# First attention: two of four key blocks turned by VectorE and DRAM, and twelve weight units split on GpSimd during the first up-projection

## The chip, the cores and the metric

One core of a Trainium2 chip. The metric is the time of one execution of the program in microseconds (us); lower is better. The engines are called by their names in the profile: PE (TensorE, the matrix unit; PEld is its weight loads), DVE (VectorE), ACT (ScalarE), POOL (GpSimd) and SP (SyncE, which here only issues DMAs). SBUF is the on-chip memory of 128 partitions, PSUM holds the results of matmuls, DRAM is the memory off the core.

## What is computed

One layer of an encoder over two batches of 512 tokens ("prompt" and "sample"), width 1024: half a SwiGLU feed-forward, a mixing block (attention beside an mLSTM memory, merged by gates), half a second feed-forward, and a norm.

```python
def encoder_layer(x, cos, sin, ...):
    x = x + 0.5 * swiglu(rms_norm(x, ffn1_norm), ffn1_w_gate, ffn1_w_up, ffn1_w_down)
    h = rms_norm(x, mix_norm)
    proj = h @ w_in
    aq, ak, av, mq, mk, mv, gate_pre, o_pre, g_att, g_mlstm = jnp.split(proj, split_at, axis=-1)
    aq = apply_rope(rms_norm(aq.reshape(B, S, ATT_HEADS, ATT_HEAD_DIM), q_norm), cos, sin)
    ak = apply_rope(rms_norm(ak.reshape(B, S, ATT_KV_HEADS, ATT_HEAD_DIM), k_norm), cos, sin)
    att = gqa_block_attention(aq, ak, av)      # softmax(q k^T / 8) v: 8 heads of 64, 2 key/value heads
    mem = mlstm_bidirectional(mq, mk, mv, gate_pre, mlstm_gate_bias, o_pre, mlstm_head_norm)
    merged = jax.nn.sigmoid(g_att) * (att @ w_up_att) + jax.nn.sigmoid(g_mlstm) * (mem @ w_up_mlstm)
    x = x + merged @ w_out
    return x + 0.5 * swiglu(rms_norm(x, ffn2_norm), ffn2_w_gate, ffn2_w_up, ffn2_w_down)
```

Everything is float32. The feed-forward's inner width is 2816, which the kernel cuts into 22 blocks of 128.

## The kernel before

**Number format.** A float32 operand is split into a rounded high part and the rest, its low part; a product is then three matmuls (high by high, high by low, low by high). The split of a tile takes two instructions: one that writes the high part (ACT, L278, L332, L715) and a subtraction that writes the low part (DVE, L279, L333, L716).

**Stages.** In the trace of before: a prologue to about 84 us; the first up-projection (`Up.rest`, its products at L374) from 84 to 437; the first down-projection to 652; the mixing block, first for the prompt (s = 0), then for the sample (s = 1); and the second feed-forward from about 1390 to the end. The first attention (prompt) runs from 705 to 813, the second (sample) from about 1081 to 1187.

**Order of work.** The order of PE's matmuls is the order of the program, pinned. The other engines' instructions are put in order by a scheduler from priorities, and each engine then takes its own list strictly in that order, waiting on semaphores. DMAs are issued from SP's list, and some from POOL's.

**First up-projection.** Both batches go through it together: each block of the 22 is made of seven products, each of twelve matmuls (L374), except that for every second block two of the products were made and kept earlier. So its pattern repeats every two blocks. DVE forms sums and differences of weights (L355), splits them (L333, L716), and reads the products' sums out of PSUM (L413, L418); the raw weights come by SP (L271). Its tiles come from a ring with several named groups; the group "o" has seven tiles, which hold outputs until they are joined. POOL has hardly any work here: `mix_gains`, called after block 13, loads the gains of the norms.

**Weight units of the mixing block.** `in_w` is used in units of 1024 x 128 (512 KB). `load_w` (L285) brings a unit for the first batch raw (SP, L271), splits it by ACT (L278) and DVE (L279) into a pair of high and low tiles, and writes both to DRAM ("wpark", two DMAs of SP at L303). For the second batch it reads the two parts back (two DMAs, L293), with no split. A unit's matmuls are handed out in steps ("fillers") between the pieces of the attention: `among(n)` issues n steps (their lines are L825, L839 and L804).

**First attention.** Head by head (8), and in a head four passes, b = 0 to 3, one for each block of 128 queries. A pass makes for the next head the score (PE, L1101, 128 queries x 512 keys), its maximum (DVE, L1104), the exponential (ACT, L1106) and the scaling by the reciprocal of the sum (ACT, L1109, or DVE, L1111). For the present head it turns one block of 128 keys with `turn_keys`: four transposes of 128x128 on PE (L1117) into PSUM, which `parts` splits (ACT L715, DVE L716), for two matmuls with the values (L1148) one pass later. The second attention does so with two of the four key blocks only. The other two (key blocks 0 and 1) are turned by DVE in blocks of 32x32 (`turn_early`, L1129) into a tile "box", sent to DRAM by SP (`send`, L1133: four DMAs of 128 KB), and fetched in the turned order by POOL (`fetch`, L1138), two passes or more later; the blocks come in the order 2, 3, 0, 1.

Of the kernel before, what the change touches and what calls it, by code (L numbers as in the profile page):

```python
# [8 lines left out]
F32 = mybir.dt.float32  # L9
F32R = mybir.dt.float32r  # L10
I32 = mybir.dt.int32
AF = mybir.ActivationFunctionType
ALU = mybir.AluOpType
# [3 lines left out]
P = 128  # L17
S = 512
D = 1024
KD = D // P  # L20
# [6 lines left out]
def encoder(ctx, tc, I, outs):  # L27
    nc = tc.nc
    cpool = ctx.enter_context(tc.tile_pool(name="cpool", bufs=1))
    dpool = ctx.enter_context(tc.tile_pool(name="dpool", bufs=1, space=bass.MemoryType.DRAM))  # L30
# [11 lines left out]
    def nm(s):  # L42
        n_id[0] += 1
        return f"{s}_{n_id[0]}"

    @contextmanager
    def shifted(n):

        tc.cur_priority += n
        yield  # L50
        tc.cur_priority -= n
# [31 lines left out]
    class Rings:  # L83
# [11 lines left out]
        def rest(self, kind):  # L95

            rows = self.rows[kind]
            i = self.at[kind] % len(rows)
            return rows[i:] + rows[:i]
# [184 lines left out]
    parked = {}  # L284
# [24 lines left out]
    G_ = nc.gpsimd  # L309
    HK_ = KD // 2  # L310
# [156 lines left out]
    class Up:  # L467
# [13 lines left out]
        def fetch(self, j, which=(0, 1), behind=None):  # L481
            return [fetch_w(self.v[i][:, :, j * P:(j + 1) * P], behind) for i in which]
# [18 lines left out]
        def left(self, j):  # L501
            return gu_left_a(self.fetch(j, (0,))[0])

        def rest(self, raw, at=None, hook=None):
            ring = self.ring

            def resume(j):
                got = ring("v"), ring("h")
                for t, d in zip(got, self.kept.pop(j)):
                    nc.sync.dma_start(t, d)  # L510
                return got

            left = gu_left_b(*raw, ring)
            left.update(gu_left_c(raw[1], ring))
            raw = self.fetch(self.order[1])
            got = resume(self.order[0])
            for i, j in enumerate(self.order):
                W = left
                nxt = self.order[i + 1] if i + 1 < NF else None
                if nxt is not None:  # L520
                    left = {} if nxt in self.kept else gu_left_a(raw[0])
                    left.update(gu_left_b(*raw, ring))
                    ru = raw[1]
                    raw = self.fetch(self.order[i + 2]) if i + 2 < NF else None
                then = []
                h = gu_rest(W, self.xc, got, ring, lambda: then.append(resume(nxt)) if nxt in self.kept else None)
                got = then[0] if then else None
                if nxt is not None:
                    left.update(gu_left_c(ru, ring))
                if i % 2 == 0:  # L530
                    sides = Sides(self.rb[i // 2], ring)
                    with shifted(LATER):
                        sides.even(*h)
                elif i < NF - 1:
                    sides.odd(*h)
                if i == at:
                    hook(h[0])
            ring.join("o", "o", "wd")
            return lambda: sides.odd(*h)

# [178 lines left out]
    HA, HK, DA = 8, 2, 64  # L719
    HM, DM = 4, 128  # L720
# [44 lines left out]
    win_v = w_in.rearrange("(k p) c -> p k c", p=P)  # L765
# [82 lines left out]
    def mix(s, xh, xl, early=None, extra=None, after=None):  # L848
# [248 lines left out]
        def score(h, b):  # L1097
            hk = h // 4
            p = PS()
            for j in range(2):  # L1100
                pin(nc.tensor.matmul(p, qT[:, h, b * P:(b + 1) * P], kv[:, hk * 2 + j, :],  # L1101
                                     start=(j == 0), stop=(j == 1)))
            c = small(3, "asm")
            V_.tensor_reduce(c[:, 0:1], p, axis=AX.X, op=ALU.max, negate=True)  # L1104
            e = T2()
            nc.scalar.activation(e, p, AF.Exp, bias=c[:, 0:1], accum_out=c[:, 1:2])  # L1106
            V_.reciprocal(c[:, 2:3], c[:, 1:2])
            if b % 2 and (s or h or b < 3):
                nc.scalar.activation(e, e, AF.Copy, scale=c[:, 2:3])  # L1109
            else:  # L1110
                V_.tensor_scalar(e, e, c[:, 2:3], None, op0=ALU.mult)  # L1111
            return e

        def turn_keys(Ps, kb):
            p = PT()
            for b in range(4):
                pin(nc.tensor.transpose(p[:, b * P:(b + 1) * P], Ps[b][:, kb * P:(kb + 1) * P], ident))  # L1117
            return parts(p.rearrange("p (i a m) -> p a i m", i=4, a=4) if s else p)

        def parts(p):  # L1120
            ph, pl = T2(F32R), T2(F32R)
            v = (lambda t: t.rearrange("p (a i m) -> p a i m", i=4, a=4)) if len(p.shape) > 2 else lambda t: t
            split(p, v(ph), v(pl))
            return ph, pl
# [3 lines left out]
        def turn_early(t, b):  # L1128
            V_.transpose(turned[:, :, b, :], t[:, 0:2 * P].rearrange("p (n m) -> p n m", m=32))  # L1129
# [6 lines left out]
        def fetch(h, kb):  # L1136
            p = F2()
            nc.gpsimd.dma_start(p, abuf[h % 2][4 * kb:4 * kb + 4].rearrange("c r a x -> (c r) (a x)"))  # L1138
            return parts(p)

        pos = {}
        KBS = (2, 3, 0, 1) if s else (0, 1, 2, 3)

        def values(h, kb, pp):
            if kb == KBS[0]:
                pos[h] = PO()
            for i, w in enumerate(pp):
                pin(nc.tensor.matmul(pos[h], Vst[:, kb, h // 4, :], w, start=(kb == KBS[0] and i == 0),  # L1148
                                     stop=(kb == KBS[3] and i == 1)))
            if kb != KBS[3]:  # L1150
                return
            po = pos.pop(h)
            order = ((lambda t: t.rearrange("p (a i m) -> p i a m", i=4, a=4)),
                     (lambda t: t.rearrange("p (i a m) -> p i a m", i=4, a=4))) if s else (lambda t: t,) * 2
            if h % 2 == 0:
                afs[0] = T2(F32, "f2")
            af = afs[0]
            o0 = (h % 2) * DA
            o1 = DA - o0
            t = T2(F32, "f2")  # L1160
            was, now = order
            nc.scalar.activation(now(t[o0:o0 + DA, :]), was(po[o1:o1 + DA, :]), AF.Copy)
            V_.tensor_tensor(now(af[o0:o0 + DA, :]), was(po[o0:o0 + DA, :]), now(t[o0:o0 + DA, :]), op=ALU.add)
            if h % 2:
                split(af, att[:, h // 2, 0, :], att[:, h // 2, 1, :])
# [18 lines left out]
        Ps = []  # L1184
        rope = q_rope(1)
        for b in range(4):
            Ps.append(score(0, b))
            next(rope, None)
            among(FIRST[b])
        if s:  # L1190
            for i in range(2):
                turn_early(Ps[i], i)
        last = None
        for h in range(HA):
            nxt = []
            for b in range(4):
                if h in (0, 2, 4) and b == 2:
                    q_turn(h // 2 + 1, pin)
                if (h, b) == (0, 1):
                    gate_tops(*tops)  # L1200
                if (h, b) in ((0, 3), (2, 3)):
                    rope = q_rope(h // 2 + 2)
                if h < 4:
                    next(rope, None)
                if h + 1 < HA:
                    nxt.append(score(h + 1, b))
                if s and (h, b) != (HA - 1, 3) and b in (3, 0):
                    if b == 3:
                        for i in range(2):
                            turn_early(nxt[i], i)  # L1210
                    else:
                        for i in range(2, 4):
                            turn_early(Ps[i], i)
                if s and b == 1:
                    send(h)
                n0, n1_ = FILLER if b else SOON
                among(n0)
                pp = None
                if not s or b > 1:
                    pp = h, b, turn_keys(Ps, b)  # L1220
                elif h:
                    pp = h - 1, b, fetch(h - 1, b)
                among(n1_)
                if last:
                    values(*last)
                last = pp
                if extra and b == 2 and h in (2, 3, 4):
                    extra[h - 2]()
            Ps = nxt
        for b in range(2 * s):  # L1230
            pp = HA - 1, b, fetch(HA - 1, b)
            among(sum(FILLER))
            values(*last)
            last = pp
# [145 lines left out]
        if s:  # L1380
# [3 lines left out]
            at = [mem_blocks(0, mem_head(0))]  # L1384
# [71 lines left out]
    up = Up(xc, I["ffn1_w_gate"][0], I["ffn1_w_up"][0], rbuf[0], 12)  # L1456
# [245 lines left out]
    for k in range(HK_):  # L1702
# [10 lines left out]
        if k == 2:  # L1713
            raw0 = up.fetch(up.order[0])
# [2 lines left out]
    up.begun()  # L1717


    tail = up.rest(raw0, 13, mix_gains)  # L1720
    accs = [None, None]
    nhl = [None, None]
    box()
# [89 lines left out]
    up = Up(xc, I["ffn2_w_gate"][0], I["ffn2_w_up"][0], rbuf[1], 10)  # L1813
    raw0 = up.fetch(0)
# [20 lines left out]
    tail = up.rest(raw0)  # L1835
# [120 lines left out]
```

## Time and profile before

The median of three runs is 2034.01 us (2033.39 to 2034.31). The execution that was profiled took 2037.6 us, and its span, from the first to the last instruction recorded, is 2035.8 us, at a granted PE clock of 0.999.

| engine | busy us | share of the span | instructions |
|---|---|---|---|
| PE | 2020.2 | 99% | 9185 |
| PEld | 1665.7 | 82% | 9185 |
| DVE | 1584.0 | 78% | 2828 |
| ACT | 921.5 | 45% | 1675 |
| POOL | 111.1 | 5% | 148 |

A row of the stretches gives the us of the stretch, each engine's busy time with its instructions, the granted clock, the share of time in which the DMA engines were busy, and GB/s. In rows by line, "out<-in" are the program's tile names, "| busy, mean ns |" are the total in us and the mean of one in ns, and what follows is the engine's idle time just before, with what ended it. A row of the timeline begins with start and duration in us; "x12" counts neighbouring instructions, and a bracket holds the wait before it.

### The profile page before, as it was taken

Reading aid. Unit: us, or ns where it says so; the run is one execution under the profiler, and the core shown is the slowest. Engines: PE = TensorE matmul, PEld = TensorE weight load, DVE = VectorE, ACT = ScalarE, POOL = GpSimd, SP = SyncE. Lnnn points to the kernel's source line nnn. Section 1 sums busy time; section 2 is a strip of 40 time slices with the busy share of each in tenths; the row PEclk is TensorE's granted clock in tenths of the full one; section 3 lists DMA queues with packets and bytes.
Section 4 is the critical chain, followed back from the end, with each engine's and each line's share of the span. In section 5 each row is a group of like instructions: output and inputs, shape, how many; then the busy total and the mean of one; then the engine's idle time right before and its main releaser. Section 6 shows DMA issues by size and latency. Waiting matters only on the chain.

```text
span 2035.8 us, 26777 instructions
## 1 busy us (share of the span) xinstructions
PE 2020.2 (99%) x9185; PEld 1665.7 (82%) x9185; DVE 1584.0 (78%) x2828; ACT 921.5 (45%) x1675; POOL 111.1 (5%) x148
## 2 busy tenths in 40 slices
PE   9999999999999999999999999999999999999998
PEld 7888888888888888888888877888888888888887
DVE  7988888886797798776566867467798988786797
ACT  7644444442234577653325654245444444442224
POOL 0000000001003000100120000011000000000001
PEclk9999999999999999999999999999999999999999
DMA  9656565799766954868656668877565655689753
GB/s 312 197 171 216 177 218 182 237 334 364 271 214 225 294 169 148 259 208 302 211 166 209 214 189 268 274 228 228 173 206 166 217 177 179 205 332 352 269 196 119
DMA packets 334696, 462.17 MB, mean 227 GB/s; under 512 B 21384, under 2 KB 207840, under 8 KB 333280
## 3 DMA queue, kind: packets, MB, share of 16 engines
q1 hardware_dynamic: 329920, 446.08, 65.8%
q0 software_dynamic: 4480, 14.11, 2.0%
q8 instruction: 72, 1.18, 0.2%
q14 instruction: 64, 0.52, 0.1%
q10 hardware_dynamic: 160, 0.27, 0.0%
HBM read 292.44 MB, written 167.94 MB: 226 GB/s over the span
## 4 chain that ended last, share of the span: by engine, by line
PE 91%; DVE 3%; DMA 3%; ACT 2%; issue 1%; SPq 0%; DVEq 0%; ACTq 0%
PE mm L839 13%; PE pso L374 12%; PE pst L374 12%; PE mm L374 10%; PE mm L632 9%; PE pss L374 6%; PE pst L632 4%; PE pss L632 4%; PE mm L825 4%; PE mm L804 3%; PE pso L632 3%; PE pso L1148 1%; PE pss L1101 1%; PE pst L839 1%; PE pss L839 1%; PE pso L1360 1%
## 5 line engine op out<-in xcount | busy, mean ns | idle before, releaser
L374 PE MATMUL pst<-xc,w 128*128 128x512 f32 x1056 | 253.8, 389 | 1.2 <-ACT t L409 1.2
L374 PEld LDWEIGHTS pst<-xc,w 128*128 128x128 f32 x1056 | 198.1, 188 | 42.7 <-ACT t L409 1.6
L374 PE MATMUL mm<-xc,w 128*128 128x512 f32 x972 | 229.6, 390 | 1.6 <-ACT f L382 1.6
L374 PEld LDWEIGHTS mm<-xc,w 128*128 128x128 f32 x972 | 182.0, 188 | 39.6 <-ACT f L382 2.1
L632 PE MATMUL mm<-rt,w 128*128 128x512 f32 x765 | 178.7, 389 | 0.0
L839 PE MATMUL mm<-xh,w 128*128 128x512 f32 x560 | 176.1, 391 | 1.4 <-DMA w<-wpark 1.4
L332 ACT ACTIVATE w<-t 128x512 fp32r<-128x512 f32 x176 | 106.5, 627 | 135.7 <-issue 63.1
L632 PEld LDWEIGHTS mm<-rt,w 128*128 128x128 f32 x765 | 143.5, 188 | 29.8
L333 DVE TENSOR_TENSOR w<-t,w 128x512 fp32r<-128x512 f32 x176 | 117.8, 688 | 40.9 <-ACT w L332 39.1
L374 PE MATMUL pso<-xc,f 128*128 128x512 f32 x528 | 127.0, 389 | 0.0
L374 PE MATMUL pss<-xc,w 128*128 128x512 f32 x528 | 126.8, 389 | 0.0
L374 PE MATMUL pso<-xc,w 128*128 128x512 f32 x528 | 126.8, 389 | 0.0
L839 PEld LDWEIGHTS mm<-xh,w 128*128 128x128 f32 x560 | 104.8, 188 | 23.7 <-DMA w<-wpark 1.8
L374 PEld LDWEIGHTS pso<-xc,f 128*128 128x128 f32 x528 | 99.0, 188 | 21.0 <-DVE t L413 0.4
L374 PEld LDWEIGHTS pso<-xc,w 128*128 128x128 f32 x528 | 99.1, 188 | 20.6
L374 PEld LDWEIGHTS pss<-xc,w 128*128 128x128 f32 x528 | 99.1, 188 | 20.6
L825 PE MATMUL mm<-xh,w 128*128 128x512 f32 x336 | 111.9, 398 | 0.0
L839 PE MATMUL mm<-xl,w 128*128 128x512 f32 x280 | 109.6, 391 | 0.0
L715 ACT ACTIVATE w<-wr 128x512 fp32r<-128x512 f32 x72 | 45.1, 632 | 138.4 <-PE pso L632 64.8
L278 ACT ACTIVATE w<-wr 128x1024 fp32r<-128x1024 f32 (+1 forms) x64 | 65.3, 1030 | 80.4 <-issue 24.5
L279 DVE TENSOR_TENSOR w<-wr,w 128x1024 fp32r<-128x1024 f32 (+1 forms) x64 | 79.8, 1247 | 26.6 <-ACT w L278 15.7
L715 ACT ACTIVATE w<-t 128x512 fp32r<-128x512 f32 x82 | 51.8, 632 | 107.4 <-PE pst L632 62.4
(457 smaller groups left out, 4080.4 us busy)
## 6 DMA issues: line engine op xcount, KB each, us to landing
rt<-rbuf SPq DMA_DIRECT2D x154, 512.0 KB, 5.4
wpark<-w SPq DMA_DIRECT2D x88, 512.0 KB, 3.6
w<-wpark SPq DMA_DIRECT2D x88, 512.0 KB, 5.3
wr<-in_ffn_w_gate_dram SPq DMA_DIRECT2D x62, 512.0 KB, 5.4
rbuf<-tab SPq DMA_DIRECT2D x102, 256.0 KB, 4.0
wr<-in_ffn_w_up_dram SPq DMA_DIRECT2D x44, 512.0 KB, 4.6
rbuf<-f SPq DMA_DIRECT2D x72, 256.0 KB, 4.2
wr<-in_w_in_dram SPq DMA_DIRECT2D x36, 512.0 KB, 5.7
```

What stands on the lines that cost most here:

```text
L278: pin(nc.scalar.activation(hi, raw, AF.Copy))
L279: pin(lo_eng.tensor_tensor(lo, raw, f(hi), op=ALU.subtract))
L332: pin(nc.scalar.activation(t[:, 0], src, AF.Copy))
L333: pin(V_.tensor_tensor(t[:, 1], src, f(t[:, 0]), op=ALU.subtract))
L374: nc.tensor.matmul(p, a[:, k, :], xt[:, b, k, :], start=(first and k == 0 and i == 0), stop=(k == HK_ - 1 and i == 2), skip_group_check=True)
L632: nc.tensor.matmul(p, u[:, a, d * P:(d + 1) * P], r[:, b, ts], start=(first and q == 0 and k == 0), stop=(q == len(us) - 1 and k == 2), sk ...
L715: nc.scalar.activation(hi, src, AF.Copy)
L804: mark(nc.tensor.matmul(p[b][:, :N], a[:, k, bs], w_[:, kl, :], start=(k == 0 and i == 0), stop=(k == KD - 1 and i == 2)), (kl, b, i) == ( ...
L825: pin(nc.tensor.matmul(p[0], a[:, k, :], b, start=(k == 0 and i == 0), stop=(k == n - 1 and i == 2)))
L839: mark(nc.tensor.matmul(p, a[:, k, :], b, start=(k == 0 and i == 0), stop=last), last)
L1101: pin(nc.tensor.matmul(p, qT[:, h, b * P:(b + 1) * P], kv[:, hk * 2 + j, :], start=(j == 0), stop=(j == 1)))
L1148: pin(nc.tensor.matmul(pos[h], Vst[:, kb, h // 4, :], w, start=(kb == KBS[0] and i == 0), stop=(kb == KBS[3] and i == 1)))
```

## The change

Two parts.

First, the attention of the prompt is written as that of the sample: for heads 0 to 6, key blocks 0 and 1 go by `turn_early`, `send` and `fetch`; the last head, 7, still turns all four by PE (2 and 3 in its passes, 0 and 1 behind them). The blocks come in the order 2, 3, 0, 1. All scaling of heads 1 to 7 is on ACT.

Second, twelve units of `in_w`, those whose steps are issued around the first attention, are split during the first up-projection by POOL: in 24 pieces of half a unit (256 KB), each with one load, a rounding copy, a subtraction and two stores to wpark, through two tiles that are taken out of the group "o" (five are left). Two pieces stand behind each block in the code. At s = 0 these units are then read like those of the second batch: two DMAs from wpark, and no split.

```diff
-        def rest(self, raw, at=None, hook=None):
+        def rest(self, raw, at=None, hook=None, aside=()):
             ring = self.ring
+            if aside:
+                spare = [ring.rows["o"].pop(4) for _ in range(2)]
+
+            def split_aside(view, d):
+                lo, hi = [t.rearrange("p (k c) -> p k c", c=P) for t in spare]
+                nc.gpsimd.dma_start(lo, view)
+                G_.tensor_copy(hi.bitcast(F32R), lo)
+                G_.tensor_tensor(lo.bitcast(F32R), lo, hi, op=ALU.subtract)
+                for i, t in enumerate((hi, lo)):
+                    nc.gpsimd.dma_start(d[:, i], t)
...
                 if i == at:
                     hook(h[0])
+                for piece in aside[2 * i:2 * i + 2]:
+                    split_aside(*piece)
...
-            if b % 2 and (s or h or b < 3):
+            if b % 2 and (s or h or b < 3) or not s and h:
                 nc.scalar.activation(e, e, AF.Copy, scale=c[:, 2:3])
...
-            return parts(p.rearrange("p (i a m) -> p a i m", i=4, a=4) if s else p)
+            return parts(p.rearrange("p (i a m) -> p a i m", i=4, a=4))
...
-        KBS = (2, 3, 0, 1) if s else (0, 1, 2, 3)
+        KBS = 2, 3, 0, 1
...
-        if s:
-            for i in range(2):
-                turn_early(Ps[i], i)
+        for i in range(2):
+            turn_early(Ps[i], i)
...
-                if s and (h, b) != (HA - 1, 3) and b in (3, 0):
+                if b in (3, 0) and h + b // 3 < (HA - 1 if not s else HA):
...
-                if s and b == 1:
+                if b == 1 and (h < HA - 1 or not (not s)):
                     send(h)
...
-                if not s or b > 1:
+                if b > 1:
                     pp = h, b, turn_keys(Ps, b)
                 elif h:
                     pp = h - 1, b, fetch(h - 1, b)
...
-            Ps = nxt
-        for b in range(2 * s):
-            pp = HA - 1, b, fetch(HA - 1, b)
+            Ps = nxt or Ps
+        for b in range(2):
+            pp = HA - 1, b, turn_keys(Ps, b) if not s else fetch(HA - 1, b)
...
-    tail = up.rest(raw0, 13, mix_gains)
+    pieces = []
+    for c in (896, 1408, *(2832 + d * P for d in range(2)), *(2320 + h * P for h in range(HM)),
+              *(2832 + d * P for d in range(2, 6))):
+        shape = [P, 2, KD, P]
+        d = dpool.tile(shape, F32, name=nm("wpark"))
+        parked["in", c] = d, shape
+        for a in range(2):
+            ks = slice(a * HK_, (a + 1) * HK_)
+            pieces.append((win_v[:, ks, c:c + P], d[:, :, ks]))
+    tail = up.rest(raw0, 13, mix_gains, pieces)
```

How the instructions stand on three engines, before and after (each engine's list is taken strictly in this order; the numbers behind the names are those of the buffers). POOL, in the first up-projection: before, the gains of `mix_gains` follow right behind a store of the prologue's kept products.

```order
L1636 DMA kept_0_291<-t_8_269 128x512
L733 COPY gain_97<-t_15_276 128x8
L735 DMA gain_97<-in_mix_norm_dram 128x8x1
L735 DMA gain_98<-in_ffn_norm_dram 128x8x1
L736 DMA gbias<-in_mlstm_gate_bias_dram 128x16
L737 DMA hn<-in_mlstm_head_norm_dram 128x4x1
```

After, the pieces stand between them; this is the first piece and the beginning of the second.

```order
L1647 DMA kept_0_291<-t_8_269 128x512
L511 DMA tab_284<-in_w_in_dram 128x4x128
L512 CAST tab_284<-tab_284 128x512
L513 TENSOR_TENSOR tab_284<-tab_284 128x512
L515 DMA wpark_1008<-tab_284 128x512 x2
L511 DMA tab_284<-in_w_in_dram 128x4x128
```

All 24 pieces stand there in one row, on the same two tiles, ahead of the gains; nothing in POOL's list ties a piece to a block of PE's, so it runs as fast as its own DMAs and instructions let it.

PE, in the first attention, head 2, between its passes 1 and 2 (L825 are steps of a unit's projection, L908 turns the queries of the next pair of heads, L1101 is a score): before, a pass holds a group of four transposes ahead of the two matmuls with the values.

```order
L1117 MATMUL pst_6285<-ident,t_515_6101 128x128
L1117 MATMUL pst_6285<-ident,t_527_6145 128x128
L1117 MATMUL pst_6285<-ident,t_534_6175 128x128
L1117 MATMUL pst_6285<-ident,t_540_6204 128x128
L825 MATMUL mm_6222<-xh_4898,w_6113 128x512 x2
L825 MATMUL mm_6222<-xl_4899,w_6113 128x512
L1148 MATMUL pso_6297<-t_552_6259,kv_5279 128x512
L1148 MATMUL pso_6297<-t_553_6260,kv_5279 128x512
L908 MATMUL mm_6300<-ident,mg_5283 128x128 x4
L1101 MATMUL pss_6309<-kv_5279,qT_5282 128x512 x2
```

After, at the same place (L837 are the steps, L1160 the values, L920 the turned queries, L1113 the scores).

```order
L837 MATMUL mm_6303<-xl_5031,w_6203 128x512
L837 MATMUL mm_6303<-xh_5030,w_6203 128x512 x2
L837 MATMUL mm_6303<-xl_5031,w_6203 128x512
L1160 MATMUL pso_6317<-t_542_6340,kv_5411 128x512
L1160 MATMUL pso_6317<-t_543_6341,kv_5411 128x512
L920 MATMUL mm_6376<-ident,mg_5415 128x128 x4
L1113 MATMUL pss_6385<-kv_5411,qT_5414 128x512 x2
```

Fourteen such groups of four transposes are gone from PE's list, passes 0 and 1 of seven heads; the values' matmuls stay, with an operand that came by DRAM.

DVE, in the same head: before, the split of a unit (L279) and a scaling (L1111) stand among the maxima and the splits of turned keys.

```order
L1104 TENSOR_REDUCE asm_6202<-pss_6199 128x1
L872 TENSOR_TENSOR mg_5283<-mm_6119,R_5150 128x512
L1107 RECIPROCAL asm_6202<-asm_6202 128x1
L279 TENSOR_TENSOR w_6216<-wr_6214,w_6216 128x1024
L1104 TENSOR_REDUCE asm_6241<-pss_6238 128x1
L716 TENSOR_TENSOR t_547_6230<-pst_6224,t_546_6229 128x512
L1107 RECIPROCAL asm_6241<-asm_6241 128x1
L1111 TENSOR_SCALAR t_550_6243<-t_550_6243,asm_6241 128x512
```

After, four block turns stand there, and the split at L728 reads a tile f, which POOL fetched from DRAM.

```order
L728 TENSOR_TENSOR t_536_6311<-pst_6305,t_535_6310 128x512
L1141 STREAM_TRANSPOSE box_5410<-t_509_6191 128x8x32
L1141 STREAM_TRANSPOSE box_5410<-t_517_6225 128x8x32
L1116 TENSOR_REDUCE asm_6323<-pss_6320 128x1
L1141 STREAM_TRANSPOSE box_5410<-t_523_6255 128x8x32
L1141 STREAM_TRANSPOSE box_5410<-t_531_6288 128x8x32
L1119 RECIPROCAL asm_6323<-asm_6323 128x1
L1116 TENSOR_REDUCE asm_6350<-pss_6347 128x1
L728 TENSOR_TENSOR t_543_6341<-f_541_6338,t_542_6340 128x512
```

In all, against before: on PE 56 transposes fewer; on DVE 28 block turns more, 12 splits of 128x1024 (L279) and 14 scalings (L1111) fewer; on ACT 12 copies of 128x1024 (L278) fewer and 14 scalings (L1109) more; on POOL 24 rounding copies and 24 subtractions of 128x512 more, and 86 DMAs more; on SP 16 DMAs more (36 fewer for the units' loads and stores, 24 more for their reads, 28 more for the sends).

More of the change, by code (lines that the diff above doesn't have):

```diff
@@ L1153, in values @@
             order = ((lambda t: t.rearrange("p (a i m) -> p i a m", i=4, a=4)),
-                     (lambda t: t.rearrange("p (i a m) -> p i a m", i=4, a=4))) if s else (lambda t: t,) * 2
+                     (lambda t: t.rearrange("p (i a m) -> p i a m", i=4, a=4)))
             if h % 2 == 0:
```

## The prediction, made before the changed kernel ran

> **What bounds the kernel now.** I read the page's list of busy times first, then the stretches of the two stages that the change touches, then single rows in them.
>
> ```profile
> PE 2020.2 (99%) x9185; PEld 1665.7 (82%) x9185; DVE 1584.0 (78%) x2828; ACT 921.5 (45%) x1675; POOL 111.1 (5%) x148
> 200.00:320.00 120.00, 120.00 (x531) 99.38 (x530) 101.85 (x160) 52.93 (x89) 0.00 (x0) 1.00 0.58 190
> 320.00:437.00 117.00, 117.00 (x516) 96.57 (x516) 101.32 (x161) 49.30 (x84) 4.00 (x6) 1.00 0.76 253
> 720.00:780.00 60.00, 59.87 (x304) 48.89 (x303) 54.92 (x118) 44.36 (x88) 0.00 (x0) 1.00 0.47 158
> 780.00:835.00 55.00, 55.00 (x272) 44.61 (x271) 42.42 (x84) 40.57 (x82) 2.04 (x1) 1.00 0.53 184
> ```
>
> PE works in 120.00 of 120.00 us of the first up-projection and in 114.87 of 115.00 us of the first attention, at full granted clock. So a matmul taken away there shortens the run by its time, and a matmul that has to wait lengthens it by the wait. Nothing else sets the end, but DVE is near behind: 85% in the up-projection (101.85 of 120) and 92% in the attention's middle (54.92 of 60). The question is whether the other engines still keep PE fed.
>
> The order of the instructions shows that the change does what it says: in PE's list 14 groups of four transposes are gone, and POOL's list has 24 pieces, in a row. So "nothing happens" is not among the rivals. Two terms are left: a gain in the attention, and a cost in the up-projection.
>
> **The attention: what goes.** PE's timeline, in the first attention:
>
> ```profile
> 744.38 0.60 PE L1117 MATMUL pst<-ident,t 128*128 128x128 f32 x4
> 744.73 0.48 PE L825 MATMUL mm<-xh,w 128*128 128x512 f32 x1
> 745.04 0.63 PE L1148 MATMUL pso<-t,kv 128*128 128x512 f32 x2
> ...
> 97.64 2.72 PE mm L374 x12
> 130.28 2.72 PE mm L374 x12
> ```
>
> Durations overlap on PE, so I go by starts. A 128x512 matmul takes 2.72 / 12 = 0.227 us (chain of waits, twelve in a row). From the transposes' start to the values' start there are 745.04 − 744.38 = 0.66 us with one such matmul in between, so a group of four costs 0.66 − 0.227 = 0.43 us. 14 x 0.43 = **6.1 us less on PE**.
>
> The other engines gain room as well. The groups by line, over the whole run:
>
> ```profile
> L279 DVE TENSOR_TENSOR w<-wr,w 128x1024 fp32r<-128x1024 f32 (+1 forms) x64 | 79.8, 1247 | 26.6 <-ACT w L278 15.7 <-DMA wr<-in_w_out_dram 9.7 <-DMA wr<-in_w_in_dram 0.5
> L1129 DVE STREAM_TRANSPOSE box<-t 128x256 f32<-128x256 f32 x32 | 12.7, 424 | 0.9 <-ACT t L1109 0.8
> L1111 DVE TENSOR_SCALAR t<-t,asm 128x512 f32<-128x512 f32 x33 | 16.0, 485 | 0.8
> L1109 ACT ACTIVATE t<-t,asm 128x512 f32<-128x512 f32 x31 | 22.3, 719 | 1.4 <-DVE asm L1107 1.2
> L278 ACT ACTIVATE w<-wr 128x1024 fp32r<-128x1024 f32 (+1 forms) x64 | 65.3, 1030 | 80.4 <-issue 24.5 <-PE mm L839 12.9 <-PE mm L804 11.3
> ```
>
> DVE: 12 splits of 1.247 less (−15.0), 14 scalings of 0.485 less (−6.8), 28 block turns of 0.424 more (+11.9): −9.9 us. ACT: 12 copies of 1.030 less (−12.4), 14 scalings of 0.719 more (+10.1): −2.3 us. Around the attention neither becomes the bound.
>
> What the change adds there are 14 waits for a fetch. Behind the wait stand the two splits (ACT, then DVE), and behind DVE's split the next maxima, which free the scores' PSUM for PE. The second attention already runs in this way, and its stretches show what it costs:
>
> ```profile
> 1080.00:1120.00 40.00, 40.00 (x192) 32.83 (x191) 29.26 (x74) 24.97 (x54) 2.86 (x5) 1.00 0.65 197
> 1120.00:1160.00 40.00, 39.35 (x189) 32.09 (x188) 34.83 (x83) 27.51 (x56) 3.78 (x7) 1.00 0.67 208
> 1160.00:1190.00 30.00, 29.89 (x139) 24.08 (x138) 18.00 (x41) 17.78 (x40) 2.13 (x4) 1.00 0.53 162
> ...
> f<-abuf POOLq DMA_DIRECT2D x16, 256.0 KB, 4.1
> abuf<-box SPq DMA_DIRECT2D x32, 128.0 KB, 2.5
> ```
>
> PE is idle there for 0.65 + 0.11 = 0.76 us of 110, against 0.13 in the first attention's two stretches, so I give back about 0.5 us: **−5.6 us**. The send stands in pass 1 of a head and its first fetch in pass 0 of the next, three passes on. The attention's 108 us (705 to 813) make 32 passes of 3.4 us, so some 10 us lie between, and send and fetch need 2.5 + 4.1 = 6.6. SP's list gets four sends a head more, but loses the twelve raw loads and 24 stores: level. The bounds of this term: −6.1 (nothing given back) and +3, where each of the 14 fetches makes PE wait as long as the one wait of the second attention (0.65): −6.1 + 9.1.
>
> **The up-projection: what a piece costs.** The pieces are on POOL, idle there (0.00 us of 120), and their DMAs are beside the others. Raw traffic is no bound: a piece moves 0.25 + 0.5 MB, 24 of them 18.9 million bytes; in the time worked out below that is 70 GB/s on top of 190, and the row 320 to 437 shows 253 GB/s with PE at 117.00 of 117.00. The gains of `mix_gains` come later by all that is left of the pieces, but POOL's next work stands at 467.88, after 134.76 us of idling:
>
> ```profile
> 467.88 0.60 POOL L744 DMA_DIRECT2D tab<-in_c_tri_dram  x1 [134.76 <-DMA wr<-in_ffn_w_down_dram]
> ```
>
> That hides them. The ring "o" with five tiles instead of seven I put at nothing, as the stores of its tiles land in some 4 us and a tile comes round again only after several sums.
>
> What is not hidden is that POOL's and DVE's instructions hinder each other. POOL has done such subtractions once, six of them, in the merge behind the first attention (timelines of POOL and DVE; the first and the last of six):
>
> ```profile
> 964.51 1.30 POOL L716 TENSOR_TENSOR ml<-mg,mh 128x512 fp32r<-128x512 f32 x1 [78.41 <-ACT mh L715]
> 981.98 1.28 POOL L716 TENSOR_TENSOR ml<-mg,mh 128x512 fp32r<-128x512 f32 x1 [1.89 <-ACT mh L715]
> ...
> 964.99 1.37 DVE L716 TENSOR_TENSOR xl<-f,xh 128x512 fp32r<-128x512 f32 x1 [1.22 <-ACT xh L715]
> 966.88 0.68 DVE L716 TENSOR_TENSOR xl<-f,xh 128x512 fp32r<-128x512 f32 x1
> 982.47 1.34 DVE L1274 TENSOR_TENSOR mg<-mg,t 128x512 f32<-128x512 f32 x1
> ```
>
> The DVE instruction that meets a POOL subtraction takes 1.37 and 1.34 instead of 0.68, and ends 0.55 us behind POOL's end. It loses 0.69 and 0.66 us to POOL's 1.30 and 1.28: about **half of what POOL runs**.
>
> POOL's time for a piece: a subtraction of 1.29 (the two rows above) and a copy of 128x512 that the trace doesn't show. Its nearest rows:
>
> ```profile
> L218 POOL COPY fold<-fold 128x96 f32<-128x96 f32 x1 | 0.3, 264 | 0.1
> L733 POOL COPY gain<-t 128x8 f32<-128x8 f32 x1 | 0.2, 184 | 285.4 <-DVE t L438 285.4
> ```
>
> 80 ns for 88 more elements are 0.91 ns each, so 512 take about 0.64 us (bounds: 0.26, the row itself, and 1.29, as dear as the subtraction). A piece holds POOL for 1.93 us, all 24 for **46.3 us** (37.2 to 61.9).
>
> How long they last: on one pair of tiles a piece must load, wait for a DVE instruction under way (0.69), compute, issue and store before the next can load.
>
> ```profile
> x2buf<-f POOLq DMA_DIRECT2D x16, 256.0 KB, 3.9
> f<-tbuf POOLq DMA_DIRECT2D x16, 256.0 KB, 6.7
> L1138 POOL DMA_DIRECT2D f<-abuf x16 | 8.8, 552 | 96.2 <-DVE asm L1104 33.8 <-DVE t L716 19.9 <-DMA abuf<-box 19.7
> ```
>
> 4.1 (the fetch's row above) + 0.69 + 1.93 + 0.55 + 3.9 = 11.2 us, 24 times: 268 us, so the stage of 353 us holds them all. The pattern of PE repeats every 130.28 − 97.64 = 32.64 us (two blocks), so that is 8.2 periods. With transfers of 2.5 it is 184 us, 5.6 periods; with 6.7, 398 us, 12.2 periods (the stage has 10.8).
>
> How much DVE can give: two of its waits in a period, one for ACT and one for PE, don't depend on how DVE itself is doing.
>
> ```profile
> 204.30 0.69 DVE L355 TENSOR_TENSOR t<-wr 128x512 f32<-128x512 f32 x1 [1.83 <-DMA wr<-in_ffn_w_up_dram]
> 208.06 1.23 DVE L333 TENSOR_TENSOR w<-wr,w 128x1024 fp32r<-128x1024 f32 x1 [1.13 <-ACT w L332]
> 211.92 0.69 DVE L418 TENSOR_TENSOR t<-t,pst 128x512 f32<-128x512 f32 x1 [1.31 <-PE pst L374]
> ```
>
> 1.13 + 1.31 = 2.44 us a period can be lost by DVE without PE seeing it. The 1.83 I leave out, since that load is issued only when DVE has freed its buffer, so the wait moves along with DVE. Over 8.2 periods DVE can give **20.0 us**.
>
> What DVE loses: at least half of 46.3, by the six rows, and at most 46.3 times the share of its time in which it runs instructions that can be hit. I take these to be those with both inputs in SBUF. Those that read PSUM:
>
> ```profile
> L405 DVE TENSOR_TENSOR t<-t,pss 128x512 f32<-128x512 f32 x8 | 5.4, 681 | 0.0
> L418 DVE TENSOR_TENSOR t<-t,pst 128x512 f32<-128x512 f32 x7 | 4.8, 687 | 5.2 <-PE pst L374 5.2
> L413 DVE TENSOR_TENSOR t<-t,pso 128x512 f32<-128x512 f32 x7 | 4.8, 684 | 0.0
> L423 DVE TENSOR_TENSOR t<-t,pso 128x512 f32<-128x512 f32 x7 | 4.8, 682 | 0.0
> ```
>
> (101.85 − 19.8) / 120 = 68%. Between half and 68% I take the middle, 59%: 27.3 us lost, 20.0 given, **+7.3 us** on PE. The bounds: nothing, if the holds fall into waits (a gain has no way here, PE being at 120.00 of 120.00), and 46.3 − 20.0 = 26.3, if every hold stops DVE. Along the other unknowns, at 59%: a hold of 37.2 gives +1.9, of 61.9 +16.5; with 5.6 periods +13.6, with 10.8 +1.0.
>
> [...]
>
> **The sum.** −5.6 + 7.3 = **+1.7 us**. The profiled execution of 2037.6 (span 2035.8) would become 2039.3; it lies 3.6 above the median of the runs, 2034.0, to which I add the same: **2035.7 us**.
>
> **The rivals.**
>
> 1. *The holds fall into waits, or end before DVE's next fitting instruction; the up-projection costs nothing.* For it: DVE is idle for 15% of the stage, 4.9 us a period, and my sum uses 2.44 of them. Against it: DVE waits in few places, and POOL's pieces come when their DMAs land. It gives 2034.0 − 5.6 = **2028.4**. The run comes out faster by over 0.2% (4.1 us, about what a measurement of this kernel can tell from no change) when the loss stays under 21.5 us, 46% of the hold.
> 2. *DVE becomes the bound of the up-projection: the collisions cost as much as their share of time.* At 68% the loss is 31.5, +11.5 on PE, and the sum +5.9: **2039.9**; with a longer copy, or shorter transfers, up to 2046. It decides above a loss of 29.7 us, 64% of the hold, where the run is slower by over 0.2%. For it: DVE runs back to back for most of a period, so a hold finds it at work. Against it: the six rows show half.
> 3. *The fetched quarters come late in the first attention.* The price is +3 for the term instead of −5.6, so **2044.3** with the up-projection as forecast. Against it: the second attention, built alike, shows 0.76 us of idle PE.
>
> **How the numbers follow.** The forecast, a loss between 46% and 64%, within 0.2% of before: 0.42. Rival 1: 0.26, faster. Rival 2: 0.26 and rival 3: 0.06, both slower. So faster 0.26, same 0.42, slower 0.32. The forecast's own range is 2030 to 2038. The range for 8 in 10 goes down to 2027.5, past rival 1 and the whole 6.1, and up to 2046, which takes in rival 2 and the longer copy (+16.5 − 5.6 = +10.9, 2044.9) and leaves out the hold that always stops DVE (2054.7).
>
> **What would show it.** In the profile after: PE's share in the stretches between 84 and 437, and the stage's end (437 before; 444 by my sum, 437 by rival 1, 449 by rival 2); DVE instructions of about 1.3 us instead of 0.69 in that stage, some two in a piece; POOL's copy near 0.64 and its pieces every 11 us, the last near 355; in the attention a stage some 5.6 us shorter with PE idle for under 1 us. I am wrong if PE waits for fetches (more than 3 us in that stage), if the pieces take other than 180 to 350 us, or if DVE loses much less or more than 27 us to them.

## The result, and the profile after

The changed kernel takes **2064.35 us** (median of 4, 2061.45 to 2066.18) against 2034.16 before (median of 4): a ratio of **1.014, 95% interval 1.0127 to 1.0152**, 30.2 us slower. The forecast was 2035.7, the range 2027.5 to 2046. The profiled execution took 2064.84 us, 27.2 more than that of before.

The page of after, its busy times and the shares by engine of the chain that ended last:

```profile
PE 2018.7 (98%) x9129; PEld 1662.5 (81%) x9129; DVE 1589.9 (77%) x2830; ACT 919.7 (45%) x1677; POOL 229.3 (11%) x282
...
PE 79%; DMA 10%; POOL 4%; DVE 3%; issue 2%; ACT 1%; SPq 0%; POOLq 0%; DVEq 0%; ACTq 0%
```

PE was 91% of that chain before. Now 14% of it is DMA and POOL (3% before): for a stretch the end hangs on the pieces. The stretches of the up-projection after (columns as before) show which:

```profile
84.00:200.00 116.00, 116.00 (x512) 95.73 (x511) 104.71 (x154) 49.13 (x83) 43.36 (x46) 1.00 0.72 234
200.00:320.00 120.00, 119.15 (x526) 97.96 (x525) 109.04 (x159) 52.85 (x89) 41.10 (x44) 1.00 0.75 243
320.00:437.00 117.00, 88.12 (x378) 72.22 (x377) 75.34 (x117) 37.01 (x64) 27.27 (x35) 0.87 0.62 203
```

Until 320 us PE has lost 0.85 us. Then it stands still for 29 us, once, and the granted clock falls to 0.87 in the mean. PE's waits over the whole run (engine, line, what it waited for: us in total, times, longest) hold one of that size:

```profile
PE pso L374 <- DVE t L423: 28.9, 1, 28.9
PE pss L1303 <- DVE t L1319: 1.7, 4, 0.7
PE pst L1454 <- DVE xc L1539: 1.6, 1, 1.6
PE mm L851 <- DMA w<-wpark: 1.4, 1, 1.4
PE mm L374 <- ACT t L382: 0.9, 1, 0.9
```

What DVE was waiting for is in its own timeline, and behind that stands POOL's. The timelines of after, PE, DVE and POOL:

```profile
349.23 2.88 PE L374 MATMUL pst<-xc,w 128*128 128x512 f32 x12
381.00 4.63 PE L374 MATMUL pso<-xc,w 128*128 128x512 f32 x10 [28.88 <-DVE t L423]
...
342.18 0.69 DVE L415 TENSOR_TENSOR t<-t,t 128x512 f32<-128x512 f32 x1
377.00 0.69 DVE L418 TENSOR_TENSOR t<-t,pst 128x512 f32<-128x512 f32 x1 [34.12 <-POOL gain L745]
380.26 0.68 DVE L423 TENSOR_TENSOR t<-t,pso 128x512 f32<-128x512 f32 x1
...
77.44 0.78 POOL L511 DMA_DIRECT2D tab<-in_w_in_dram  x1 [37.66 <-ACT xc L319]
374.47 1.25 POOL L513 TENSOR_TENSOR tab<-tab 128x512 fp32r<-128x512 f32 x1
375.67 1.10 POOL L515 DMA_DIRECT2D wpark<-tab  x2
376.76 0.20 POOL L745 COPY gain<-t 128x8 f32<-128x8 f32 x1
```

Read from the end: PE may not write `pso` before DVE has read it at L423; that stands in DVE's list behind L418; and L418 waits 34.12 us, until a POOL copy that itself takes 0.20 us. The copy is the first instruction of `mix_gains`. It is there to hold the loads of the gains back until block 13 is made, and does so by reading eight columns of that block's tile h. As long as it has not read, DVE may not write that tile again, and L418 of a later block is what writes it next. POOL reaches the copy only behind all 24 pieces, at 376.76 us. Before (timelines of POOL, DVE and PE), the copy ran 19 us ahead of L418, and PE's product began without a wait:

```profile
323.59 0.18 POOL L733 COPY gain<-t 128x8 f32<-128x8 f32 x1 [285.43 <-DVE t L438]
...
342.53 0.69 DVE L418 TENSOR_TENSOR t<-t,pst 128x512 f32<-128x512 f32 x1 [1.36 <-PE pst L374]
...
350.44 2.88 PE L374 MATMUL pso<-xc,w 128*128 128x512 f32 x12
```

The pause costs more than its length, as stretches of after behind it show:

```profile
381.00:386.00 5.00, 5.00 (x12) 3.97 (x13) 5.00 (x9) 2.72 (x6) 0.59 (x1) 0.52 0.92 258
386.00:392.00 6.00, 6.00 (x27) 4.70 (x27) 6.00 (x11) 2.39 (x5) 0.00 (x0) 1.00 0.99 339
```

For 5 us the granted clock is 0.52, and twelve matmuls need that long where they need 2.72 at a granted 1.00. In the 6 us after that the clock is 1.00 again.

To see where the rest went I laid the two traces over each other: the median, over stretches of 30 us, of how much later the same instructions of DVE and ACT start than before. The difference of that shift across a stage is what the stage costs. For after, and for the experiments below (one profiled execution each; that of before lies 3.6 us above its median, so the columns compare stages, not whole runs):

| kernel | first up-projection (90 to 570 us) | first attention and what stands beside it (660 to 870) |
|---|---|---|
| after | +32.8 | −5.0 |
| e1_hook18 | +4.5 | −4.5 |
| e3_copy_act | +1.2 | −5.1 |
| e4_att_only | −0.3 | +1.8 |
| e5_pieces18 | +2.8 | −1.6 |
| e6_eleven | +11.4 | −2.6 |
| e7_copies | +7.2 | −4.7 |
| e8_dma_only | −0.3 | −3.8 |
| e9_eight | +1.0 | −0.1 |
| e10_dve_split | +20.6 | −1.8 |
| e11_two_pairs | +2.6 | −2.0 |

For after: 28.9 for the pause and 2.5 for the slow matmuls behind it (PE's next three products begin at 381.00, 386.04, 388.81 and the fourth at 391.69, 10.69 us for what takes 8.16), 0.9 for one wait for ACT, and half a microsecond not traced: 32.8. The attention gives back 5.0.

### The profile page after: what moved, and what is told of

The parts are those of the page before. It is cut to its first block, busy times and chain, and to the rows that moved or that the text cites. A ratio compares the mean times of both kernels' runs of the same rounds, so it can differ in the third digit from the quotient of the medians.

```text
span 2063.1 us, 26886 instructions
## 1 busy us (share of the span) xinstructions
PE 2018.7 (98%) x9129; PEld 1662.5 (81%) x9129; DVE 1589.9 (77%) x2830; ACT 919.7 (45%) x1677; POOL 229.3 (11%) x282
## 4 chain that ended last, share of the span: by engine, by line
PE 79%; DMA 10%; POOL 4%; DVE 3%; issue 2%; ACT 1%; SPq 0%; POOLq 0%; DVEq 0%; ACTq 0%
PE mm L851 14%; PE mm L644 8%; PE mm L374 8%; PE pso L374 8%; PE pst L374 7%; DMA tab<-in_w_in_dram 5%; PE mm L837 4%; PE pst L644 4%; PE pss L644 4%; DMA wpark<-tab 4%; PE pss L374 4%; PE mm L816 3%; PE pso L644 3%; POOL tab L513 2%; PE pss L1113 1%
## 5 line engine op out<-in xcount | busy, mean ns | idle before, releaser
L374 PE MATMUL pso<-xc,w 128*128 128x512 f32 x528 | 129.2, 394 | 28.9 <-DVE t L423 28.9
L374 PEld LDWEIGHTS pss<-xc,w 128*128 128x128 f32 x528 | 99.1, 188 | 20.6
L837 PE MATMUL mm<-xh,w 128*128 128x512 f32 x336 | 110.5, 395 | 0.0
L644 PE MATMUL pss<-rt,w 128*128 128x512 f32 x396 | 93.6, 389 | 0.0
L644 PE MATMUL pst<-rt,w 128*128 128x512 f32 x396 | 93.6, 389 | 0.0
```

The costliest lines, as they stand in the source:

```text
L374: nc.tensor.matmul(p, a[:, k, :], xt[:, b, k, :], start=(first and k == 0 and i == 0), stop=(k == HK_ - 1 and i == 2), skip_group_check=True)
L644: nc.tensor.matmul(p, u[:, a, d * P:(d + 1) * P], r[:, b, ts], start=(first and q == 0 and k == 0), stop=(q == len(us) - 1 and k == 2), sk ...
L837: pin(nc.tensor.matmul(p[0], a[:, k, :], b, start=(k == 0 and i == 0), stop=(k == n - 1 and i == 2)))
```

## The experiments

Theory A: the whole loss is POOL's copy in the wrong place. Theory B, that of my forecast: POOL's instructions keep DVE from its work, and PE pays for it. Every run below was timed against the kernel before on the same chip; there, before varied more than in the first runs (2032.7 to 2038.8 over all of them), so ratios are given.

**1. The gains asked for later.**

```diff
-    tail = up.rest(raw0, 13, mix_gains, pieces)
+    tail = up.rest(raw0, 18, mix_gains, pieces)
```

> Edit: the gains of the norms are asked for after block 18 of the up-projection instead of block 13; all else as in the changed kernel. Theory A (PE's one wait of 28.88 us is DVE's L418, which may not overwrite the tile h of block 13 until POOL's tiny copy of gains has read it, and that copy stands behind the 24 pieces in POOL's list): the copy now marks a tile that is not yet made at 343 us, the wait goes with the slow matmuls behind it, the stage costs under 2 us instead of 32.8, and the run takes 2028 to 2031 us. Theory B (the collisions of POOL with DVE, as forecast, cost the stage several us, and the wait only gathers what DVE is late): the stage still costs 7 us or more, 2036 us or more.

Measured: 2036.41 us, ratio 1.0001 (0.9992 to 1.001). The pause is gone. PE's waits in the stage (80 to 470 us) of this kernel, and POOL's copy:

```profile
PE mm L374 <- ACT t L382: 1.4, 2, 0.8
PE pst L374 <- ACT t L409: 0.9, 1, 0.9
PE pso L374 <- DVE t L413: 0.5, 2, 0.3
...
398.23 0.59 POOL L745 COPY gain<-t 128x8 f32<-128x8 f32 x1 [18.10 <-DVE t L444]
```

POOL now waits for the tile, not DVE for POOL. The wait did not come back elsewhere, so A holds for 28 us. But the run is not at 2028 to 2031: the stage still costs 4.5 us, between the two expectations, of which 2.8 are listed as small waits of PE for ACT and DVE. Whether that rest is B's, with a smaller term, this run can't tell; runs 6 and 7 ask.

**2. The attention's part alone** (the changed kernel without the list of pieces).

```diff
-    tail = up.rest(raw0, 13, mix_gains, pieces)
+    tail = up.rest(raw0, 13, mix_gains)
```

> Edit: the attention's part of the change alone; no pieces, so the twelve units are split by ACT and DVE during the attention as before. Theory A (transposes taken off a full PE are worth their time, 5.05 us in the attention of the changed kernel): 2028 to 2030 us. Rival (DVE, 92% busy there before, now has 11.9 - 6.8 = 5.1 us more instead of 9.9 less, so without the pieces the turns come late and PE waits for them): the gain is lost, 2033 us or more, with waits of PE for DVE in the stage.

Measured: 2038.06 us, ratio 1.0016 (1.0007 to 1.0025), slower. Here theory A's expectation missed, and the rival was right. PE's waits from 690 to 860 us in this kernel, where before has none:

```profile
PE pso L1160 <- DVE f L1175: 1.8, 3, 1.2
PE pso L1160 <- DVE t L728: 1.5, 4, 0.9
PE pso L816 <- DVE f L1175: 1.5, 1, 1.5
PE pss L1303 <- DVE t L1319: 0.5, 1, 0.5
```

The transposes are gone from PE, yet the stage is 1.8 us longer: PE waits for DVE, which has 28 turns more and all its unit splits. That DVE's load alone makes it late is not shown. In this stretch (700 to 850) the fetches land in 5.3 us in the median, against 4.1 in e3_copy_act, beside 240 GB/s against 212, and ACT, whose half of a split comes ahead of DVE's, waits 1.9 us for two of them (e3_copy_act has no such wait). Without the pieces ACT's copies and the units' DMAs stay too, and no run takes these apart.

**3. The pieces alone** (before, with the changed kernel's `rest` and its list of pieces, the gains after block 18).

> Edit: the pieces alone, with the gains asked for after block 18; the attention as before. Theory A (the collisions fall into DVE's waits): the up-projection costs about 1 us, the attention is PE's own time and gains nothing from the relief of DVE: 2033.5 to 2036 us. Theory B (collisions as forecast): up-projection plus 7 us, 2039 to 2043 us.

Measured: 2037.20 us, ratio 1.0008 (0.9999 to 1.0017). The time lies between the two theories' ranges. The up-projection costs 2.8 us, and the attention's stage gains 1.6 from the relief alone, where theory A expected nothing. Runs 2 and 3 together: +1.8 and −1.6 apart, about −5 jointly. The gain needs both parts.

**4. Eleven units instead of twelve**, gains still after block 13.

```diff
-              *(2832 + d * P for d in range(2, 6))):
+              *(2832 + d * P for d in range(2, 5))):
```

> Edit: eleven units instead of twelve go to POOL, 22 pieces, with the gains still asked for after block 13. Theory A: POOL's copy of the gains comes when the 22nd piece is issued, at 358.7 instead of 376.8 us, so PE's wait is 28.9 - 18.1 = 10.8 us and the run 2046 us (2043 to 2049). Theory B (the cost is that of collisions, spread over the pieces): a twelfth of the 30 us goes, 2061.8 us.

Measured: 2048.07 us (2044.15 to 2050.29), ratio 1.006 (1.0047 to 1.0073). The rows of this kernel (PE's wait, POOL's copy, PE's timeline):

```profile
PE pso L374 <- DVE t L423: 7.1, 1, 7.1
...
354.08 0.20 POOL L745 COPY gain<-t 128x8 f32<-128x8 f32 x1
...
358.31 5.34 PE L374 MATMUL pso<-xc,w 128*128 128x512 f32 x12 [7.06 <-DVE t L423]
```

Two pieces fewer bring the copy forward from 376.76 to 354.08, 22.7 us, and PE's wait goes down from 28.9 to 7.1, by 21.8. A twelfth of the pieces carries three quarters of the pause: it is a matter of when, as A says, not of how much POOL does.

**5. The copy by ACT instead of POOL**, after block 13 as in the changed kernel.

```diff
-        pin(nc.gpsimd.tensor_copy(gm, behind[:, 0:KD]))
+        pin(nc.scalar.activation(gm, behind[:, 0:KD], AF.Copy))
```

> Edit: as the changed kernel, gains still asked for after block 13, but the tiny copy that reads block 13's tile h (128x8) is ACT's and not POOL's. Theory A (only the place of that copy in POOL's list makes PE wait): PE's wait of 28.9 us is gone although nothing else moved, 2034 to 2039 us, like the run with block 18. Rival (block 18 helped by another way, such as a later start of the gains' loads, or DVE is late by itself): PE still waits near 350 us, 2050 us or more.

Measured: 2035.62 us, ratio 1.0007 (0.9998 to 1.0015). PE's waits in the stage (80 to 470 us) are now one:

```profile
PE mm L374 <- ACT t L382: 0.5, 1, 0.5
```

One instruction of 128x8 changes its engine, and 28 us are gone. That leaves theory A alone for the pause.

**6 and 7. What the rest of the stage's cost is**: the copy of each piece made twice, and no arithmetic on POOL at all.

```diff
-                G_.tensor_copy(hi.bitcast(F32R), lo)
+                for _ in range(2):
+                    G_.tensor_copy(hi.bitcast(F32R), lo)
```

> Edit: as e3_copy_act, and POOL makes each rounding copy twice (same values). Theory C (what is left of the stage's cost, 4.5 us with block 18, is POOL's instructions standing in DVE's way): with about 1 us more of POOL in each of 24 pieces the stage costs 3 to 10 us more, 2039 to 2046 us. Theory D (it is the pieces' DMA traffic): unchanged against e3_copy_act within 2 us.

```diff
-                G_.tensor_copy(hi.bitcast(F32R), lo)
-                G_.tensor_tensor(lo.bitcast(F32R), lo, hi, op=ALU.subtract)
-                for i, t in enumerate((hi, lo)):
+                for i, t in enumerate((lo, lo)):
```

> Edit: as e3_copy_act, without POOL's copy and subtraction; each piece is loaded and its raw values stored twice, so these twelve units' high and low parts are both the raw weights at s = 0 and s = 1 (this part of the computation is left out). Theory C (collisions): the stage costs under 1.5 us and the run is 3 us or more below e3_copy_act, 2031 to 2034 us. Theory D (traffic): the stage still costs 3 us or more, 2034 to 2038 us.

Measured: 2040.75 us (ratio 1.0032, 1.0019 to 1.0044) with the doubled copies, 2034.76 us (0.9998, 0.9989 to 1.0007) with DMAs alone. Run 6 fits theory C in its time and in its stage. The time of run 7 does not: it is only 0.9 us under run 5, where C said 3 or more, and lies in theory D's range. Its stage decides, as D wants a cost of 3 us or more there and it shows none (−0.3). In the same execution the attention gains less (3.8), and 3.3 us are lost behind the second attention. Stretches of before, e3_copy_act, e7_copies and e8_dma_only, one fence each:

```profile
84.00:437.00 353.00, 353.00 (x1558) 291.99 (x1557) 301.88 (x475) 151.89 (x257) 4.00 (x6) 1.00 0.63 207
```

```profile
84.00:437.00 353.00, 352.50 (x1552) 290.48 (x1551) 323.76 (x475) 151.62 (x257) 109.86 (x122) 1.00 0.78 258
```

```profile
84.00:437.00 353.00, 349.23 (x1530) 285.88 (x1528) 321.39 (x463) 149.37 (x251) 140.74 (x146) 1.00 0.76 251
```

```profile
84.00:437.00 353.00, 353.00 (x1559) 292.40 (x1558) 302.07 (x477) 152.29 (x257) 45.43 (x74) 1.00 0.79 259
```

With POOL's arithmetic, the same 475 DVE instructions are busy for 323.76 us instead of 301.88: 21.9 us lost. With the same DMAs at 259 GB/s and no arithmetic, DVE loses nothing and PE is at 353.00 of 353.00. In these executions the traffic is free, and POOL's arithmetic is not. The groups of POOL in e3_copy_act show the other side of them:

```profile
L513 POOL TENSOR_TENSOR tab<-tab 128x512 fp32r<-128x512 f32 x24 | 45.6, 1900 | 2.1
...
L512 POOL CAST tab<-tab 128x512 fp32r<-128x512 f32 x24 | 23.0, 960 | 99.0 <-DMA tab<-in_w_in_dram 99.0
```

POOL is held up as well: its subtraction takes 1.90 us in the mean (1.25 at its shortest in after), the copy 0.96 (0.61).

**8. Eight units on POOL.**

```diff
-    for c in (896, 1408, *(2832 + d * P for d in range(2)), *(2320 + h * P for h in range(HM)),
-              *(2832 + d * P for d in range(2, 6))):
+    for c in (896, 1408, *(2832 + d * P for d in range(2)), *(2320 + h * P for h in range(HM))):
```

> Edit: as e3_copy_act, with eight units (16 pieces) on POOL instead of twelve; the last four are split by ACT and DVE in and behind the attention. If the stage's cost goes with the pieces, it is 3.0 instead of 4.5 us. If the attention's gain needs only DVE's relief up to its last heads, most of its 4.5 us stays: 2034 to 2036 us, the fastest of these. If every unit of relief is needed, a third of the way to the attention's part alone is lost (it was 1.8 us slower in its stage): 2036 to 2038 us.

Measured: 2037.23 us, ratio 1.001 (1.0001 to 1.0019). The stage costs 1.0, but the attention's gain falls to 0.1: by this one execution, the last four units' relief carries nearly all of it. The other kernels stand between: with no unit relieved the attention's stage loses 1.8 us (run 2), with eight it gains 0.1, with ten 2.0 (run 10), with eleven 2.6 and 1.8 (runs 4 and 9), with twelve 3.8 to 5.1.

**9 and 10. A version that should win: the pieces split by ACT and DVE, spread over the blocks.** In 10 with two pairs of tiles, so that loads are issued two pieces ahead.

```diff
-                G_.tensor_copy(hi.bitcast(F32R), lo)
-                G_.tensor_tensor(lo.bitcast(F32R), lo, hi, op=ALU.subtract)
+                nc.scalar.activation(hi[:, 0, 0:1].bitcast(F32R), behind[:, 0:1], AF.Copy)
+                nc.scalar.activation(hi.bitcast(F32R), lo, AF.Copy)
+                V_.tensor_tensor(lo.bitcast(F32R), lo, hi, op=ALU.subtract)
```

> Edit: as e3_copy_act, but the pieces (22, eleven units, one a block) are split by ACT (copy) and DVE (subtraction) in their place among the block's work; POOL only issues their DMAs. A tiny ACT copy from the block's tile h holds a piece until its block. Theory C (POOL's 68.6 us of instructions took 21.9 us from DVE in e3_copy_act's stage): DVE pays 22 x 0.6 = 13.2 us instead, under the 20 us that it can give, so the up-projection costs under 1 us, the attention gains 4 to 5, and the run is 2031 to 2034 us. Rival (ACT or DVE, which now stand in their own lists behind a piece's load, wait for its DMA where pieces lie only 10 us apart, and PE pays): 2035 us or more, with DVE or ACT waiting for the pieces' load in the profile.

> Edit: as e10_dve_split with ten units (20 pieces) and two pairs of tiles in turn, so that a piece's load is issued two pieces ahead (the ring o keeps three tiles). Theory C, with e10_dve_split's loss put down to loads that landed late where two pieces lie 10 us apart: ACT no longer waits for the pieces' loads (43.8 us there, now under 3), DVE's extra 20 x 0.6 = 12 us stay under the 20 it can give, the up-projection costs under 1.5 us, the attention (ten of twelve units relieved) gains 2 to 4: 2031 to 2035 us. Rival (three tiles of o are too few and their stores hold DVE up, or ACT's order is what hurts): 2037 us or more, with DVE or ACT waiting for stores or for each other.

Measured: 2054.38 us (ratio 1.0086, 1.0072 to 1.0099) and 2040.21 us (1.0023, 1.0014 to 1.0032). In the first the rival was right. ACT's waits in its stage begin with

```profile
ACT tab L514 <- DMA tab<-in_w_in_dram: 43.8, 11, 8.6
```

an instruction that stands in ACT's list ahead of a load that has not landed, and behind it ACT's work for PE. With two pairs of tiles this row is gone and the stage costs 2.6 us instead of 20.6, so the loads were the main cost. Theory C's time was missed all the same, and the run lies in the rival's range: the stage costs more than the 1.5 us forecast, with ten of twelve units relieved the attention gains only 2.0, and 2.6 us more come late in the second attention and the merge, where I did not trace them further. Whether it was the rival's mechanism is not shown. No version that I ran beats the kernel before.

## Why the prediction was wrong

**The step that failed** is this one: "The gains of `mix_gains` come later by all that is left of the pieces, but POOL's next work stands at 467.88, after 134.76 us of idling [...] That hides them." I asked who waits for what the moved instructions *write*: the gains, used late. I did not ask who waits for what they *read*. The copy holds a tile of DVE's ring until it has run, so moving it back moves DVE's L418 with it, and L418 moves PE. Rows of before had both ends: the copy at 323.59, L418 at 342.53, 19 us of slack. And the order shown with the change has `COPY gain_97<-t_15_276` with the tile that it reads in its name.

My own numbers would have given the price. I put the last piece at 355 us. L418 would then follow at 355, and PE's product 4 us later (377.00 to 381.00 in after) where PE was due at 350.44 in before: a wait of some 8.6 us and 2.5 for the slow clock. The run with eleven units is that case, with the copy at 354.08: 2048.07 us. In the changed kernel the pieces took 299 us (77.4 to 376.8, 12.5 each) instead of my 268. Most of the 31 us more stands in POOL's two instructions, recorded at 68.0 us (43.9 and 24.1) where I had 46.3; and each microsecond more went into the wait.

**The attention's term** (−5.6) was right in size: −5.0 in after, −4.5 and −5.1 in the repaired versions. Its reason was half right. I wrote that the other engines "gain room as well"; in truth that room is a condition. Without it the 6.1 us of transposes bring nothing (+1.8, run 2). PE at "114.87 of 115.00" did not show how little slack the others had. Whether the room that counts is DVE's, ACT's or the DMAs', the runs don't tell.

**The up-projection's term** (+7.3) had the right mechanism and too large a size. DVE lost 21.9 us in e3_copy_act (forecast 27.3) and gave most of it from its waits, which fell from 46.7 to 25.3 us in all (forecast 20.0); PE paid 1.2, 4.5 and 2.8 us in the three executions with all the pieces as written and no pause. What I had for POOL holds where DVE stands still, as in the pause of after: 1.25 + 0.61 = 1.86 us a piece, forecast 1.93. Beside DVE the same instructions were recorded at 68.6 us (45.6 + 23.0), above my bound of 61.9, since they are held up too. The share was the step too high: of the 46.3 us that I set against DVE it lost 21.9, or 47%, the half of the six rows and not 59%. That only DVE's instructions with both inputs in SBUF are hit, behind the 68%, was my assumption; after agrees: from 84 to 437 us the four lines that read PSUM (L405, L413, L418, L423) take 678 to 682 ns in the mean, against 681 to 687 in before, while L424 and L425, with both inputs in SBUF, take 797 and 798, against 686 and 685. At half, my own sum gives 23.2 − 20.0 = +3.2, close to what PE paid. One bound was added up wrongly as well: with transfers of 2.5 us the terms as listed give 196 us for the pieces and 6.0 periods, not 184 and 5.6, so +12.7 and not +13.6.

**The sum without the pause** comes out: e1_hook18 and e3_copy_act, the changed kernel with that one dependence mended, measure 1.0001 and 1.0007 of before, where I forecast 1.7 us, 1.0008. Part of that is luck: the up-projection cost less than forecast, the attention gained a little less, and about 1 us was lost behind the second attention, for which the sum had no term. Of the rivals none had the pause; rival 2 had the sign, for another reason.

**Open**: between the second attention and the merge the kernels with both parts lose about 1 us against before, some up to 3.9 (e9_eight), and e4_att_only, with the changed attention alone, 0.1. And why the relief alone gains 1.6 us on a PE that the profile shows as nearly full: from 690 to 750 us PE is busy for 59.75 of 60 us in before and for all 60 in e5_pieces18, and the starts of its matmuls show more pauses in before that are too short to be listed as waits, but what makes them I did not trace. Both are small against the 6.1 us over which single executions of before range.

## What to carry to other kernels

When work is put at the head of an engine's list, go through what stands behind it and ask of each instruction both who needs its result and whose buffer it holds by reading; a marker of 128x8, 0.20 us of POOL, stopped the matrix engine for 28.88 us here. An idle engine's list is only free up to the first instruction that someone else depends on. And when an edit frees one engine by loading another, test the halves alone: here neither half made the kernel faster, and the attention's 5 us came only from the pair.

## What the runs showed of the hardware

A pause of 7.06 us on PE (e6_eleven) cost as much in slow matmuls behind it as one of 28.88 (after): from start to start, the next three products took 10.70 us behind the one and 10.69 behind the other, for 8.16 normally. That is 2.5 us for either of these two pauses.

POOL's and DVE's instructions lengthened each other, where I had charged only DVE: POOL's subtraction of 128x512 took from 1.25 to 3.60 us in after, and DVE's 475 instructions in the stage took 21.9 us more in all in e3_copy_act. POOL's 72 DMAs and 18.9 MB beside the same work cost DVE nothing in e8_dma_only (302.07 us with 477 instructions, against 301.88 with 475 in before).
